# FFN input projections as one level of Strassen's product in a two-layer encoder kernel, with the weight blocks summed on GpSimd

## Chip, core and metric

The kernel runs on one core of one Trainium2 chip. The metric is the device time of one execution in microseconds (us). Before the change three runs gave 1635.26, 1635.56 and 1637.29 us; the median is 1635.56.

## What is computed

Two layers of an encoder on a sequence of 512 positions and 1024 channels, in float32. Each layer normalizes its input, projects it, runs three branches (attention, convolution, Fourier mixing), merges them through gates, projects with `w_out` and adds the residual. Then comes the feed-forward part (FFN), which the change is about:

```python
x = x + merged @ w_out[l]
h2 = rmsnorm(x, norm2_g[l])
f_gate, f_up = jnp.split(h2 @ w_ffn_in[l], 2, axis=-1)      # (512, 1024) @ (1024, 2*2816)
x = x + (jax.nn.silu(f_gate) * f_up) @ w_ffn_out[l]
```

## The kernel before

**Layout.** Activations lie transposed: a tile has 128 channels on its partitions and the 512 positions along its free side, so the 1024 channels are eight tiles (`KT`). A weight block is 128x128. All weights are packed on the host in the order of use, eight blocks to a chunk of 128x1024 elements (512 KB), 134 chunks to a layer.

**A product in float32 accuracy.** Weights and activations are split into a rounded high part and the rest. `chunk` (L185) loads a chunk to a tile `wr`, lets ScalarE (ACT) write the high part `wh` (L194) and VectorE (DVE) the rest `wl` (L195). `split` (L144) does the same for activations (L147 on ACT, L148 on DVE; with a scale L150 and L151). `gemm` (L208) multiplies one column block of weights with all tiles of the activation: for each 128-channel step three matmuls of 512 columns, high by high, high by rest and rest by high, all added up in one PSUM bank. Every matmul goes through `mm`, so all of them have line L114.

**The FFN.** After `w_out` (loop from L384, one product `ps` for each of eight tiles) the new residual `xt` is written by DVE (L391), scaled and split to the tiles `X` (L150, L151), and its squares are added up on GpSimd (POOL, L239). The inverse norm `rb2` (L420) is applied after the products. The 2816 hidden channels are 22 blocks (`NJ`); they are done in two runs of 11. For each block, called a unit here, there are two `gemm` calls with eight steps each, gate and up, which is 48 matmuls on two chunks of weights. `unit` (L399) multiplies the gate product with `rb2` (L401), applies Silu on ACT (L402), multiplies the up product with `rb2` (L404) and both together (L405), and splits the result (L147, L148). After the 11 units of a run, eight `gemm` calls with 11 steps each multiply the run's results with `w_ffn_out`, and DVE adds them to the residual (L426). So a layer has the order: `w_out`, units 0 to 10, output products, units 11 to 21, output products.

**What sets the order.** A scheduler puts the instructions of each engine into a fixed row before the program runs, by a priority that the kernel sets (`at`, with `self.t` as a running count of matmul time). Weight work is given a priority `WL` (16000 ns) ahead of its use. On the chip each engine takes its row strictly from front to back, and an instruction that has to wait holds up all behind it. Weight loads are issued from SyncE's row (SP). Tiles come from pools with a fixed number of buffers: `WB = (2, 3, 3)` for `wr`, `wh` and `wl`; a load waits until the last reader of the buffer's old content is done.

Of the kernel before, what the change touches and what calls it, by code (L numbers as in the profile page):

```python
# [9 lines left out]
F32 = mybir.dt.float32  # L10
# [6 lines left out]
P = 128  # L17
# [60 lines left out]
def lam_init(l):  # L78
    return 0.8 - 0.6 * math.exp(-0.3 * l)


class Hybrid:
# [267 lines left out]
    def main(self, l):  # L350
# [31 lines left out]
        x2, xg, acc = [], [], None  # L382
        g2 = self.par(l, "g2")
        for m in range(KT):  # L384
            xr = self.slot("M")
            self.at(self.t - 20000)
            getattr(nc, QS[3]).dma_start(xr, self.xin[m])
            self.at(self.t)
            ps = self.gemm(ms)
            xt = self.slot("V")  # L390
            nc.vector.scalar_tensor_tensor(out=xt, in0=ps, scalar=0.5, in1=xr, op0=ALU.mult, op1=ALU.add)  # L391
            xg.append(self.split_to(xt, "X", scale=g2[:, m : m + 1]))
            acc = self.sq_add(xt, acc, "M")
            x2.append(xt)
        self.xg, self.acc = [], None
        xin = []
        rb2 = None

        def unit(j, pg, pu):  # L399
            z = self.slot("M")  # L400
            nc.vector.tensor_tensor(out=z, in0=pg, in1=rb2, op=ALU.mult)  # L401
            nc.scalar.activation(z, z, AF.Silu)  # L402
            u = self.slot("M")
            nc.vector.tensor_tensor(out=u, in0=pu, in1=rb2, op=ALU.mult)  # L404
            nc.vector.tensor_tensor(out=u, in0=u, in1=z, op=ALU.mult)  # L405
# [535 lines left out]
def _pack(inp, l):  # L941
# [3 lines left out]
    def add(w):  # L945
        seq.append(_tiles(w).reshape(-1, P, P))
# [117 lines left out]
```

## Time and profile before

| | |
|---|---|
| runs | 1635.26, 1635.56, 1637.29 us |
| span of the profiled execution, first to last instruction | 1635.0 us |
| TensorE (PE) busy | 1618.7 us, 99% of the span |
| DVE busy | 1089.5 us, 67% |
| ACT busy | 678.2 us, 41% |
| POOL busy | 119.5 us, 7% |
| first layer: units 0 to 10, output products, units 11 to 21, output products | 474 to 592, to 652, to 771, to 832 us |

The own time of the profiled execution is not listed apart from its span; the median of the runs is 0.56 us above the span. Busy shares are means over stages: the units are only a part of each layer. DVE, ACT and POOL rows give the time an instruction took on its engine, including time in which it was held up after it had started. Ends of matmuls are modelled by the profiler, so the distance between two starts is what a matmul costs.

### The profile page before, as it was taken

How to read it: one execution, taken by the hardware profiler on the slowest of the kernel's cores; microseconds unless marked ns; L12 is line 12 of the kernel's file. 1: busy time of each engine (PE TensorE's matmuls, PEld its weight loads, DVE VectorE, ACT ScalarE, POOL GpSimd, SP SyncE). 2: the span in 40 equal slices, each digit the busy share in tenths (PEclk: the TensorE clock that was granted, in tenths of full speed). 3: DMA queues.
4: the chain of work that ended last, by engine and by line, in shares of the span. 5: the costliest groups of instructions: out<-in, count | busy, mean ns of one | idle time of the engine just before them, and what ended most of it. 6: DMA issues, size and time to landing. Idle time of an engine off the chain costs nothing.

```text
span 1635.0 us, 20023 instructions
## 1 busy us (share of the span) xinstructions
PE 1618.7 (99%) x7512; PEld 1340.8 (82%) x7512; DVE 1089.5 (67%) x1820; ACT 678.2 (41%) x1059; POOL 119.5 (7%) x85
## 2 busy tenths in 40 slices
PE   8999999999999999999999999999999999999999
PEld 6888888887888888888888888888878888888887
DVE  7999999896644433444459999998975444334432
ACT  5345555773443221323344464557634332223221
POOL 4000000112410000000100000001132000000000
PEclk9999999999999999999999999999999999999999
DMA  5545233322432323223343542332224223222332
GB/s 177 176 136 165 78 110 102 98 88 71 136 112 94 103 91 100 93 96 104 128 138 95 162 148 81 100 113 85 87 86 146 95 99 102 92 95 99 93 113 77
DMA packets 61439, 178.50 MB, mean 109 GB/s; under 512 B 8976, under 2 KB 9872, under 8 KB 61344
## 3 DMA queue, kind: packets, MB, share of 16 engines
q1 hardware_dynamic: 60912, 176.11, 33.3%
q0 software_dynamic: 432, 1.13, 0.3%
q8 instruction: 59, 0.97, 0.3%
q14 instruction: 36, 0.29, 0.1%
HBM read 163.30 MB, written 13.89 MB: 108 GB/s over the span
## 4 chain that ended last, share of the span: by engine, by line
PE 96%; ACT 2%; DVE 1%; DMA 0%; issue 0%; SPq 0%; DVEq 0%; ACTq 0%
PE main L114 83%; PE s L114 5%; PE att L114 3%; PE oth L114 3%; PE att L124 2%; DMA V<-in_xT 0%; PE att L583 0%; ACT at L691 0%; ACT cv L924 0%; DVE wl L195 0%; PE oth L124 0%; ACT wh L194 0%; DVE B L151 0%; ACT L924 0%; ACT L441 0%
## 5 line engine op out<-in xcount | busy, mean ns | idle before, releaser
L114 PE MATMUL main<-X,wh 128*128 128x512 f32 x2208 | 692.2, 391 | 0.0
L194 ACT CAST wh<-wr 128x1024 fp32r<-128x1024 f32 x268 | 281.7, 1052 | 649.5 <-PE main L114 375.6
L114 PEld LDWEIGHTS main<-X,wh 128*128 128x128 f32 x2208 | 413.4, 188 | 85.1 <-issue 0.5
L195 DVE TENSOR_TENSOR wl<-wr,wh 128x1024 fp32r<-128x1024 f32 x268 | 341.4, 1274 | 139.4 <-ACT wh L194 138.6
L114 PE MATMUL main<-X,wl 128*128 128x512 f32 x1104 | 431.7, 391 | 0.0
L114 PEld LDWEIGHTS main<-X,wl 128*128 128x128 f32 x1104 | 207.5, 188 | 42.7 <-issue 0.5
L867 DVE SCALAR_TENSOR_TENSOR cv<-cv,hcw,cv 128x497 f32<-128x497 f32 (+14 forms) x240 | 176.4, 735 | 1.2
L114 PE MATMUL main<-att,wh 128*128 128x512 f32 x384 | 119.6, 391 | 3.0 <-ACT att L147 3.0
L691 ACT ACTIVATE at<-s,mx 128x512 f32<-128x512 f32 x128 | 88.0, 688 | 78.6 <-DVE mx L689 63.0
L404 DVE TENSOR_TENSOR M<-main,rb 128x512 f32<-128x512 f32 x42 | 29.1, 692 | 133.8 <-PE main L114 133.8
L114 PE MATMUL main<-A,wh 128*128 128x512 f32 x320 | 106.4, 392 | 0.0
L114 PE MATMUL main<-wh,X 128*128 128x512 f32 x288 | 96.5, 391 | 0.0
L401 DVE TENSOR_TENSOR M<-main,rb 128x512 f32<-128x512 f32 x42 | 29.0, 691 | 91.0 <-PE main L114 91.0
L689 DVE TENSOR_REDUCE mx<-s 128x1 f32<-128x512 f32 x128 | 86.5, 679 | 4.3 <-PE s L114 4.0
L114 PEld LDWEIGHTS main<-att,wh 128*128 128x128 f32 x384 | 71.8, 188 | 19.2 <-ACT att L147 3.5
L114 PE MATMUL main<-act,wh 128*128 128x512 f32 x256 | 80.2, 394 | 0.0
L114 PE MATMUL main<-cv,wh 128*128 128x512 f32 x240 | 77.3, 392 | 1.1 <-ACT cv L147 1.1
L239 POOL TENSOR_TENSOR M<-M,M 128x512 f32<-128x512 f32 x28 | 46.9, 1675 | 421.0 <-ACT M L236 378.3
L114 PE MATMUL main<-att,wl 128*128 128x512 f32 x192 | 75.0, 391 | 0.0
L114 PE MATMUL main<-A,wl 128*128 128x512 f32 x192 | 74.9, 392 | 0.0
L114 PEld LDWEIGHTS main<-A,wh 128*128 128x128 f32 x320 | 59.8, 188 | 12.6 <-issue 0.5
L426 DVE TENSOR_TENSOR V<-main,V 128x512 f32<-128x512 f32 x32 | 22.1, 691 | 65.9 <-PE main L114 65.9
(223 smaller groups left out, 2260.9 us busy)
## 6 DMA issues: line engine op xcount, KB each, us to landing
wr<-in_w SPq DMA_DIRECT2D x268, 512.0 KB, 3.5
dqk<-at SPq DMA_DIRECT2D x32, 256.0 KB, 3.8
qst<-dqk SPq DMA_DIRECT2D x96, 64.0 KB, 1.9
kst<-dqk SPq DMA_DIRECT2D x96, 64.0 KB, 1.9
V<-in_xT SPq DMA_DIRECT2D x8, 256.0 KB, 7.6
att<-dftd SPq DMA_DIRECT2D x8, 256.0 KB, 4.2
M<-in_xT SPq DMA_DIRECT2D x8, 256.0 KB, 3.5
x<-V SPq DMA_DIRECT2D x8, 256.0 KB, 2.6
```

Source lines behind the costliest of these rows:

```text
L114: return self.pin(self.nc.tensor.matmul(out, lhsT=lhsT, rhs=rhs, start=start, stop=stop))
L124: self.pin(self.nc.tensor.transpose(ps[:, s], src[:, s], self.ident))
L194: nc.scalar.copy(hi, raw)
L195: nc.vector.tensor_tensor(out=lo, in0=raw, in1=hi.bitcast(F32), op=ALU.subtract)
L239: nc.gpsimd.tensor_tensor(out=sq, in0=acc, in1=sq, op=ALU.add)
L401: nc.vector.tensor_tensor(out=z, in0=pg, in1=rb2, op=ALU.mult)
L404: nc.vector.tensor_tensor(out=u, in0=pu, in1=rb2, op=ALU.mult)
L426: nc.vector.tensor_tensor(out=x2[m], in0=ps, in1=x2[m], op=ALU.add)
L689: nc.vector.tensor_reduce(out=mx, in_=ps, axis=AX.X, op=ALU.max, negate=True)
L691: nc.scalar.activation(e, ps, AF.Exp, bias=mx, accum_out=z1 if c else z0)
L867: ins = nc.vector.scalar_tensor_tensor(out=acc[:, a:b], in0=g[:, a + d : b + d], scalar=w[:, t : t + 1], in1=acc[:, a:b], op0=ALU.mult, op ...
```

## The change

The activation (1024 channels by 512 positions) and the weights of a unit (1024 by gate and up, 256 columns) are each cut into a grid of 2 by 2 blocks: channels in two halves of 512, positions in two halves of 256, weights in gate and up. One level of Strassen's product in Winograd's form then needs seven block products in place of eight, and sums of blocks before and after.

- `pair_weights` takes the place of the chunk loads of a unit. It loads the two chunks to `wr` tiles `r1` and `r2` (each holds two weight blocks of 128x512), makes three new sums `s1`, `s2`, `s4` and overwrites a part of `r1` with the fourth, `s3`. The four sums are `tensor_tensor` on GpSimd. The two `wr` tiles are split as before (`halves`), and `s1`, `s2`, `s4` are split as 128x512 tiles of their own (`single`, through `split`).
- `combine` makes the four sums of activation blocks on DVE while `w_out` is worked on, for each pair of channel tiles that belong together, and splits them. The order of the eight `w_out` products becomes 0, 4, 1, 5 and so on.
- `product` is one block product: four channel steps, three matmuls of 256 columns each. `pair_gemm` runs seven of them into two PSUM banks `b1` and `b2`. After the first four, ACT copies `b1` to `p15` and DVE adds `b2` to it; the last three are added into the banks.
- `unit` makes gate and up from `b1`, `b2` and the tile `qw` (which is `p15`) with three more sums of 256 columns.
- `WB` becomes (3, 4, 4), and weights of units get a priority 20000 ns ahead (`WLS`). Unit 0 of the first run is no longer held back until after unit 1.

The host packs the same weight blocks in another order. Line numbers of the changed kernel differ: L252 and L202 are the rest of a chunk, L154 and L155 stand for L147 and L148, L260 to L266 are the four weight sums, L281 the matmuls of `product`, L328 and L329 the copy and the sum to `p15`, L521 to L529 the DVE steps of `unit`, L509 stands for L391, and L295 to L298 are the sums of `combine`.

```diff
-WB = (2, 3, 3)
+WB = (3, 4, 4)
+WLS = 20000
+HALF = 108
...
+    def pair_weights(self, early):
...
+        self.at(self.t - WLS)
+        raws = []
+        for _ in range(2):
+            raw = self.wp.tile([P, CHUNK * P], F32, tag="raw", name=self.nm("wr"), bufs=WB[0])
...
+            nc.sync.dma_start(raw, self.a["w"][self.l, c])
...
+        r1, r2 = raws
+        a21, a11 = r1[:, 0:T], r1[:, T : 2 * T]
+        a22, a12 = r2[:, 0:T], r2[:, T : 2 * T]
...
+        g = nc.gpsimd.tensor_tensor
+        g(out=s1, in0=a21, in1=a22, op=ALU.add)
+        g(out=a21, in0=a11, in1=a21, op=ALU.subtract)
+        halves(("s3", "a11"), r1)
+        g(out=s2, in0=s1, in1=a11, op=ALU.subtract)
+        single("s1", s1)
+        single("s2", s2)
+        g(out=s4, in0=a12, in1=s2, op=ALU.subtract)
+        halves(("a22", "a12"), r2)
+        single("s4", s4)
...
+    def product(self, ps, w, xs, ks, start, stop):
...
+            for i, (a, b) in enumerate(((wh, xh), (wh, xl), (wl, xh))):
+                self.lastmm = self.pin(
+                    self.nc.tensor.matmul(
+                        ps, lhsT=a[:, s], rhs=b, start=start and k == ks[0] and i == 0,
...
+    def combine(self, ua, ub, t, tags):
...
+        v(out=t1, in0=ua[:, h:T], in1=ua[:, 0:h], op=ALU.subtract)
+        v(out=t3, in0=ub[:, h:T], in1=ua[:, h:T], op=ALU.subtract)
+        v(out=t2, in0=ub[:, h:T], in1=t1, op=ALU.subtract)
+        v(out=t4, in0=ub[:, 0:h], in1=t2, op=ALU.subtract)
...
+    def pair_gemm(self, u, w, xc, split_k=False):
...
+        first = (
+            (b1[:, 0:h], "a11", "b11", True), (b1[:, h:T], "s1", "t1", False),
+            (b2[:, h:T], "s3", "t3", True), (b2[:, 0:h], "s2", "t2", False),
+        )
...
+        p15 = self.slot("M")
+        nc.scalar.copy(p15, b1)
+        nc.vector.tensor_tensor(out=p15, in0=b2, in1=p15, op=ALU.add)
+        ks = list(range(n))
+        self.product(b1[:, 0:h], w["a12"], x("b21"), ks, False, False)
+        self.product(b1[:, h:T], w["s4"], x("b22"), ks, False, True)
+        self.product(b2[:, h:T], w["a22"], x("t4"), ks, False, True)
+        return b1, b2, p15
...
-        def unit(j, pg, pu):
+        def unit(j, b1, b2, qw):
             z = self.slot("M")
-            nc.vector.tensor_tensor(out=z, in0=pg, in1=rb2, op=ALU.mult)
+            v = nc.vector.tensor_tensor
+            v(out=z[:, 0:h], in0=b1[:, 0:h], in1=rb2[:, 0:h], op=ALU.mult)
+            v(out=z[:, h:T], in0=b1[:, h:T], in1=qw[:, 0:h], op=ALU.add)
+            v(out=z[:, h:T], in0=z[:, h:T], in1=rb2[:, h:T], op=ALU.mult)
             nc.scalar.activation(z, z, AF.Silu)
             u = self.slot("M")
-            nc.vector.tensor_tensor(out=u, in0=pu, in1=rb2, op=ALU.mult)
-            nc.vector.tensor_tensor(out=u, in0=u, in1=z, op=ALU.mult)
+            v(out=u[:, 0:h], in0=b2[:, h:T], in1=qw[:, 0:h], op=ALU.add)
+            v(out=u[:, h:T], in0=qw[:, 0:h], in1=qw[:, h:T], op=ALU.add)
+            v(out=u, in0=u, in1=rb2, op=ALU.mult)
+            v(out=u, in0=u, in1=z, op=ALU.mult)
...
-                held.append((j, self.gemm(xg, tag), self.gemm(xg, tag)))
+                w = self.pair_weights(half == 0 and j < 4)
+                got = self.pair_gemm(j, w, xc, half == 0 and j == 0)
```

Three places in the engines' fixed rows follow, of before and of the change. A name before the arrow is what is written, names behind it what is read; `main`, `s` and `att` are PSUM banks, `wr`, `wh`, `wl` weight chunks, `M` working tiles, `cv` the weight sums, `A` their split parts, `rb` the tile of `rb2`.

DVE, one unit in the first run, before: two PSUM steps, a product, a split and two chunks.

```order
L401 TENSOR_TENSOR M_5065<-main_5003,rb_4703 128x512
L195 TENSOR_TENSOR wl_5110<-wr_5107,wh_5109 128x1024
L404 TENSOR_TENSOR M_5068<-main_5034,rb_4703 128x512
L405 TENSOR_TENSOR M_5068<-M_5068,M_5065 128x512
L195 TENSOR_TENSOR wl_5151<-wr_5148,wh_5150 128x1024
L148 TENSOR_TENSOR kst_5072<-M_5068,qst_5071 128x512
```

DVE, the same place now: twelve of the fourteen steps of one round.

```order
L522 TENSOR_TENSOR M_5493<-main_5404,M_5454 128x256
L527 TENSOR_TENSOR M_5498<-M_5454 128x256
L155 TENSOR_TENSOR A_5656<-cv_5645,A_5655 128x512
L523 TENSOR_TENSOR M_5493<-M_5493,rb_4821 128x256
L526 TENSOR_TENSOR M_5498<-main_5405,M_5454 128x256
L528 TENSOR_TENSOR M_5498<-M_5498,rb_4821 128x512
L252 TENSOR_TENSOR wl_5665<-wr_5643,wh_5664 128x1024
L529 TENSOR_TENSOR M_5498<-M_5498,M_5493 128x512
L155 TENSOR_TENSOR A_5660<-cv_5646,A_5659 128x512
L252 TENSOR_TENSOR wl_5785<-wr_5775,wh_5784 128x1024
L329 TENSOR_TENSOR M_5588<-s_5539,M_5588 128x512
L155 TENSOR_TENSOR kst_5504<-M_5498,qst_5503 128x512
```

An L155 for `s4` and L521 stand ahead of the next L522 and complete the round; the step to `p15` (L329) stands right behind the chunk `wl_5785`, and only the last two rows and those two lie between that and L522.

POOL, from the last square sums of the first layer's `w_out` on, before: the next instruction belongs to the second layer.

```order
L239 TENSOR_TENSOR M_4550<-M_4508,M_4550 128x512
L239 TENSOR_TENSOR M_4592<-M_4550,M_4592 128x512
L239 TENSOR_TENSOR M_4634<-M_4592,M_4634 128x512
L239 TENSOR_TENSOR M_6671<-M_6622,M_6671 128x512
L239 TENSOR_TENSOR M_6727<-M_6671,M_6727 128x512
```

POOL, two units in the first run now: four sums to a unit with nothing between them.

```order
L260 TENSOR_TENSOR cv_5779<-wr_5775,wr_5777 128x512
L261 TENSOR_TENSOR wr_5775<-wr_5775 128x512
L263 TENSOR_TENSOR cv_5780<-cv_5779,wr_5775 128x512
L266 TENSOR_TENSOR cv_5781<-wr_5777,cv_5780 128x512
L260 TENSOR_TENSOR cv_5913<-wr_5909,wr_5911 128x512
L261 TENSOR_TENSOR wr_5909<-wr_5909 128x512
L263 TENSOR_TENSOR cv_5914<-cv_5913,wr_5909 128x512
L266 TENSOR_TENSOR cv_5915<-wr_5911,cv_5914 128x512
```

The chunk `wr_5775` is overwritten in part by the second sum, so its split (`wl_5785` in the row of DVE above) comes behind that sum.

PE, the start of a gate product before; it needs a chunk's two parts and nothing else.

```order
L114 MATMUL main_4962<-X_4630,wl_4966 128x512
L114 MATMUL main_5003<-X_4337,wh_5006 128x512 [waits DVE_49,Activation_49]
L114 MATMUL main_5003<-X_4338,wh_5006 128x512
L114 MATMUL main_5003<-X_4337,wl_5007 128x512 [waits DVE_49]
L114 MATMUL main_5003<-X_4378,wh_5006 128x512
```

PE, ahead of the seventh product of a unit now; `s_5538` and `s_5539` are its banks, `att_5672` the first bank of the next unit.

```order
L281 MATMUL s_5538<-B_4685,A_5535 128x256
L281 MATMUL att_5672<-at_4583,wh_5650 128x256 x2
L281 MATMUL att_5672<-at_4583,wl_5651 128x256
L281 MATMUL att_5672<-at_4682,wh_5650 128x256
L281 MATMUL s_5539<-X_4396,wh_5530 128x256 [waits DVE_49]
L281 MATMUL s_5539<-X_4397,wh_5530 128x256
```

The seventh product writes into `s_5539` and waits for DVE's step to `p15`, which reads that bank; a part of the next unit's first product stands ahead of it.

More of the change, by code (lines that the diff above doesn't have):

```diff
@@ new lines, in pair_gemm, with x @@
+    def pair_gemm(self, u, w, xc, split_k=False):
+        nc = self.nc
+        tag = ("s", "att", "main")[u % 3]
+        b1, b2 = self.bank(tag), self.bank(tag)
+        h = T // 2
+        n = len(xc)
+        def x(name):
+            return [p[name] for p in xc]
+        first = (
+            (b1[:, 0:h], "a11", "b11", True), (b1[:, h:T], "s1", "t1", False),
+            (b2[:, h:T], "s3", "t3", True), (b2[:, 0:h], "s2", "t2", False),
+        )
+        steps = (list(range(n - 1)), [n - 1]) if split_k else (list(range(n)),)
+        for ks in steps:
+            for i, (ps, a, b, start) in enumerate(first):
+                self.product(ps, w[a], x(b), ks, start and ks[0] == 0, i % 2 == 1 and ks[-1] == n - 1)
+        p15 = self.slot("M")
[6 more added lines that the diff above has]
+        return b1, b2, p15
@@ L381, in main @@
             ms.append(self.split_to(merged[m], "cv" if m < 4 else "A"))
-        x2, xg, acc = [], [], None
+        x2, xc, acc = [None] * KT, [], None
         g2 = self.par(l, "g2")
[L384 to L394, printed above, removed]
+        h = T // 2
+        for q in range(KT // 2):
+            us = self.wtp.tile([P, 2, T], F32, tag="wth", name=self.nm("us"))
+            ts = self.wtp.tile([P, 2, T], F32, tag="wtl", name=self.nm("ts"))
+            for i, m in enumerate((q, q + KT // 2)):
+                xr = self.slot("M")
+                self.at(self.t - 20000)
+                getattr(nc, QS[3]).dma_start(xr, self.xin[m])
+                self.at(self.t)
+                ps = self.gemm(ms)
+                xt = self.slot("V")
+                nc.vector.scalar_tensor_tensor(out=xt, in0=ps, scalar=0.5, in1=xr, op0=ALU.mult, op1=ALU.add)
+                nc.scalar.activation(us[:, i, :], xt, AF.Copy, scale=g2[:, m : m + 1])
+                acc = self.sq_add(xt, acc, "M")
+                x2[m] = xt
+            xc.append(self.combine(us[:, 0, :], us[:, 1, :], (ts[:, 0, :], ts[:, 1, :]), XCT[q]))
         self.xg, self.acc = [], None
@@ L414, in main @@
             act = []
-            held = []
             for j in range(NJ // 2):
-                tag = "s" if half == 0 and j == 0 else "main"
-                held.append((j, self.gemm(xg, tag), self.gemm(xg, tag)))
+                w = self.pair_weights(half == 0 and j < 4)
+                got = self.pair_gemm(j, w, xc, half == 0 and j == 0)
                 if half == 0 and j == 0:
                     rb2 = self.inv_rms(acc, D, "M", "rb")
-                    continue
-                while held:
-                    act.append(unit(*held.pop(0)))
+                act.append(unit(j, *got))
             for m in range(KT):
@@ L976, in _pack @@
         proj("w_proj_a", m)
-    add(inp["w_out"][l])
+    w = inp["w_out"][l]
+    for m in range(KT // 2):
+        for c in (m, m + KT // 2):
+            add(w[:, c * P : (c + 1) * P])
     w1, w2 = inp["w_ffn_in"][l], inp["w_ffn_out"][l]
@@ L980, in _pack @@
         for j in range(half * NJ // 2, (half + 1) * NJ // 2):
-            add(w1[:, j * P : (j + 1) * P])
-            add(w1[:, FF + j * P : FF + (j + 1) * P])
+            for k in range(2):
+                for o in (FF, 0):
+                    add(w1[k * D // 2 : (k + 1) * D // 2, o + j * P : o + (j + 1) * P])
         add(w2[half * FF // 2 : (half + 1) * FF // 2])
```

49 lines of the change are left out of this document (48 added, 1 removed).

## Prediction

> **What bounds the kernel now.** The page's busy times and its chain of work that ended last come first.
>
> ```profile
> PE 1618.7 (99%) x7512; PEld 1340.8 (82%) x7512; DVE 1089.5 (67%) x1820; ACT 678.2 (41%) x1059; POOL 119.5 (7%) x85
> PE 96%; ACT 2%; DVE 1%; DMA 0%; issue 0%; SPq 0%; DVEq 0%; ACTq 0%
> ```
>
> TensorE is the bound: 96% of the chain. The view by windows shows how the stages of the FFN differ from that mean: the first layer's first 11 units, and one unit alone (columns: PE, PEld, DVE, ACT, POOL busy, granted clock, DMA share, GB/s).
>
> ```profile
> 474.00:592.00 118.00, 118.00 (x520) 97.24 (x519) 57.59 (x70) 39.53 (x48) 0.00 (x0) 1.00 0.30 98
> 496.20:507.10 10.90, 10.90 (x50) 9.02 (x49) 5.04 (x6) 3.23 (x4) 0.00 (x0) 1.00 0.29 98
> ```
>
> Here PE never rests, DVE works 5.0 of 10.9 us, ACT 3.2 and POOL not at all. So fewer matmuls would shorten this stage for as long as the others can follow. The timeline of DVE in these units gives the pitch of a unit and of DVE's steps.
>
> ```profile
> 485.52 0.69 DVE L404 TENSOR_TENSOR M<-main,rb 128x512 f32<-128x512 f32 x1 [0.56 <-PE main L114]
> 486.25 0.69 DVE L405 TENSOR_TENSOR M<-M,M 128x512 f32<-128x512 f32 x1
> 486.86 1.22 DVE L195 TENSOR_TENSOR wl<-wr,wh 128x1024 fp32r<-128x1024 f32 x1
> 488.00 0.69 DVE L148 TENSOR_TENSOR act<-M,act 128x512 fp32r<-128x512 f32 x1
> ...
> 496.40 0.69 DVE L404 TENSOR_TENSOR M<-main,rb 128x512 f32<-128x512 f32 x1 [3.35 <-PE main L114]
> ...
> 507.28 0.69 DVE L404 TENSOR_TENSOR M<-main,rb 128x512 f32<-128x512 f32 x1 [3.31 <-PE main L114]
> ```
>
> A unit takes 496.40 - 485.52 = 10.88 us (507.28 - 496.40 again), which over 48 matmuls is 0.227 us for 512 columns. DVE starts an instruction before the last one has ended: after a 512-wide step of 0.69 the next starts 0.61 later (486.25 to 486.86), after a chunk of 1.22 it starts 1.14 later (486.86 to 488.00). Where a step needs the result of the one right ahead, it is 0.73 (485.52 to 486.25).
>
> **Matmuls: removed 48 of 512 columns, added 84 of 256.** Seven products of four channel steps with three matmuls are 84. The attention's second product already has 256 columns; the timeline of PE there:
>
> ```profile
> 178.56 0.29 PE L114 MATMUL att<-wtl,V 128*128 128x256 f32 x1
> 178.68 0.28 PE L114 MATMUL att<-wth,V 128*128 128x256 f32 x1
> ...
> 179.28 0.29 PE L114 MATMUL att<-wtl,V 128*128 128x256 f32 x1
> ```
>
> Start to start is 0.12 us (six steps in 0.72), more than half of 0.227. So 84 x 0.12 = 10.08 us a unit instead of 10.88: 0.80 saved, not an eighth (1.36). Over 44 units that is 35 us, if PE stays the bound.
>
> [...]
>
> **DVE: from six steps a unit to fourteen.** Counted from DVE's row of a unit: two chunks as before (2 x 1.14 = 2.28), seven steps of 512 (the rest of `s1`, `s2`, `s4` and of the activation, the sum to `p15`, `u` times `rb2`, `u` times `z`), 7 x 0.61 = 4.27, and five of 256. For these the nearest row is
>
> ```profile
> L717 DVE TENSOR_TENSOR ar<-att,ar x32: 393/412/419, 181.0 to 1198.0; 64x256 f32<-64x256 f32 x32
> ```
>
> 0.41 less the same 0.08 of overlap is 0.33 to 0.34, so 1.70. Together 8.25 us, and 8.5 with two steps that need the one right ahead (2 x 0.12). Alone DVE would still fit into 10.08.
>
> **POOL: from nothing to four sums a unit.** The source view of the branch merge has the same instruction:
>
> ```profile
> L453 POOL TENSOR_TENSOR B<-B,M x16: 1275/1289/1737, 344.8 to 1202.1; 128x512 f32<-128x512 f32 x16
> L453 POOL TENSOR_TENSOR B<-B,A x16: 1293/1672/2277, 405.5 to 1228.7; 128x512 f32<-128x512 f32 x16
> ```
>
> At 1.29 us four take 5.2, which fits. But what DVE does meanwhile is the point. First a single meeting, in the timelines of DVE and POOL, then a row of four POOL sums at the end of the branches.
>
> ```profile
> 388.55 2.31 DVE L195 TENSOR_TENSOR wl<-wr,wh 128x1024 fp32r<-128x1024 f32 x1
> 388.50 1.29 POOL L453 TENSOR_TENSOR B<-B,M 128x512 f32<-128x512 f32 x1 [7.18 <-DVE M L452]
> ...
> 406.45 1.41 DVE L195 TENSOR_TENSOR wl<-wr,wh 128x1024 fp32r<-128x1024 f32 x1
> 407.79 1.77 DVE L148 TENSOR_TENSOR cv<-B,cv 128x512 fp32r<-128x512 f32 x1
> 409.48 0.68 DVE L452 SCALAR_TENSOR_TENSOR A<-A,main 128x512 f32<-128x512 f32 x1
> 410.08 1.19 DVE L148 TENSOR_TENSOR cv<-B,cv 128x512 fp32r<-128x512 f32 x1
> 411.19 2.30 DVE L195 TENSOR_TENSOR wl<-wr,wh 128x1024 fp32r<-128x1024 f32 x1
> 405.49 6.93 POOL L453 TENSOR_TENSOR B<-B,A 128x512 f32<-128x512 f32 x4 [9.26 <-DVE A L452]
> ```
>
> A chunk of 1.22 took 2.31, longer by 1.09, because a POOL sum had started 0.05 us ahead. In the second place five DVE steps that alone take 1.14 + 3 x 0.61 + 1.22 = 4.19 us take 7.04 (406.45 to 413.49), while POOL's first sum ends and three more run whole: 2.85 more, 0.95 a sum. The two engines take turns. L452, which reads PSUM, is not held (0.68). Of DVE's fourteen steps only four read PSUM (`p15`, L521, L522, L526).
>
> [...]
>
> When do the four sums run? The second chunk of a unit's weights gets the buffer that DVE frees with the L252 right ahead of L329 (rows of the order above), and a load takes
>
> ```profile
> wr<-in_w SPq DMA_DIRECT2D x268, 512.0 KB, 3.5
> ```
>
> So the sums start about 3 us behind L329. By then L521 and L522 are through (0.61 for the activation's rest, 0.61 for `s4`, 2 x 0.34), and of the steps on PSUM only L526 falls into a sum. The sums meet the steps on SBUF: four times 1.0, less 0.34 for L526: 3.7 us. DVE's round is 8.5 + 3.7 = 12.2 us. That is over PE's 10.08, and PE's seventh product waits for L329, which stands behind all this. DVE becomes the bound, PE rests 2 us in each unit.
>
> ACT gets a copy and three casts more; with Silu and the activation's cast these are six 512-wide steps beside the two chunks:
>
> ```profile
> L194 ACT CAST wh<-wr 128x1024 fp32r<-128x1024 f32 x268 | 281.7, 1052 | 649.5 <-PE main L114 375.6
> 497.93 0.62 ACT L147 CAST act<-M 128x512 fp32r<-128x512 f32 x1 [0.70 <-DVE M L405]
> ```
>
> 2 x 1.05 + 6 x 0.62 = 5.8 us, hidden in either round. SP's row has the same 134 loads a layer, none of them behind other waits than before; DMA is busy 0.30. Free.
>
> **Which units.** The sums that run in the round of unit j are those of unit j + 3. So of 11 units in a run eight rounds have sums, the last three have none and go at PE's 10.08. A run changes by 8 x (12.2 - 10.88) - 3 x 0.80 = 10.6 - 2.4 = +8.2 us. Four runs: +32.6.
>
> **The `w_out` stage.** DVE's four sums and their splits for each pair of tiles have room except behind the last product, where before there were three steps:
>
> ```profile
> 462.89 0.69 DVE L391 SCALAR_TENSOR_TENSOR V<-main,M 128x512 f32<-128x512 f32 x1 [2.65 <-PE main L114]
> 463.79 1.22 DVE L195 TENSOR_TENSOR wl<-wr,wh 128x1024 fp32r<-128x1024 f32 x1 [0.21 <-ACT wh L194]
> 464.94 0.74 DVE L151 SCALAR_TENSOR_TENSOR X<-V,par,X 128x512 fp32r<-128x512 f32 x1
> ```
>
> That chain took 2.8 us (462.89 to 465.68). Now there are eight steps, two of 512 and one chunk, three of 256, two more of 512: 0.61 x 4 + 1.14 + 3 x 0.34 = 4.6, with 0.24 for steps in line 4.8. Unit 0 does the first three pairs of its first four products meanwhile, 36 x 0.12 = 4.3. The sums of unit 2 fall into the same time, up to 3 x 1.0. Between 0 and 3.5 us a layer; I take 3, since POOL's row has three sums there: +6 in all.
>
> **The sum.** Span 1635.0 + 32.6 + 6 = 1673.6; the median of the runs lay 0.56 above the span, so 1674.
>
> **Rivals.**
>
> *PE stays the bound.* The sums find gaps in DVE's row, a round stays under 10.08. For it: DVE was idle for over half of these units, and the meeting above shows a step on PSUM running through. Against it: with 8.5 us of its own DVE may lose no more than 1.6 a unit, 0.4 a sum, less than half of any meeting on SBUF in this trace. From that point PE decides; time 1635.6 - 35 + 6 = 1607. Chance 0.14.
>
> *The gain and the loss even out.* A loss of 0.6 a sum gives a round of 10.9, and 8 x 0.02 - 2.4 = -2.2 a run: 1635.6 - 9 + 6 = 1633, no change (within 0.2%, some 3 us, about what a measurement of this kernel can tell). Chance 0.06.
>
> *A unit's weights come late.* Load, two sums, cast and rest are a chain: 3.5 + 2 x 1.29 + 1.05 + 1.22 = 8.4 us, with two turns lost to DVE about 10. If PE had to wait for the split sums in each unit because nothing is prepared ahead, the 3.7 us that DVE loses would add to PE's 10.08 instead of lying beside it, and the round would be 13.8: 8 x 2.9 - 2.4 = 21 a run, 1635.6 + 84 + 6 = 1725. Against it: in DVE's row the split weights stand a unit ahead of their matmuls. Chance 0.10.
>
> **Chances and range.** The forecast, DVE's rounds with POOL's sums as the bound, has the remaining 0.70, nearly all of it slower. Faster by over 0.2%: 0.15; within 0.2%: 0.05; slower: 0.80. The price of a sum is between nothing (beside steps on PSUM) and its whole 1.29 us. At 0.75 a sum the round is 11.5, a run 8 x 0.62 - 2.4 = +2.6 and the time 1652; at 1.29 the round is 13.7, a run 8 x 2.8 - 2.4 = +20 and the time 1722. I reach below to 1622, which is a round of 10.6 and 0.52 a sum, and above to 1715, a round of 13.5. Left out are the fast rival and most of the late weights, under 2 in 10.
>
> **What would show it.** Right: in a unit's window PE is busy about 10 of 12.2 us, DVE without gaps, and the largest waits of the first layer's units end with L329; L252 and L155 in these units have means of 1.6 to 2.3 and near 1.2 to 1.7 us where they meet POOL, steps on PSUM keep theirs; the first run takes 474 to about 603. Matmuls of 256 columns start 0.12 apart. Wrong: PE without gaps, units of 10.1 us and DVE's means as before (the fast rival); waits of PE that end with L155 of a weight sum or with ACT's casts behind POOL (late weights); L252 unchanged beside POOL sums would break the turn-taking itself.

## The result, and the profile after

The changed kernel takes 1703.04 us (median of four runs, 1702.30 to 1704.83), the kernel before 1635.93 us beside it: a ratio of 1.0412 with a 95% interval of 1.0397 to 1.0427, 67 us slower. The forecast was 1674, its range 1622 to 1715: right in sign and mechanism, too small by 29 us. The profiled execution took 1702.3 us, 2.1 more than its span.

The page of the changed kernel, busy times and chain:

```profile
PE 1625.8 (96%) x9096; PEld 1419.3 (83%) x9096; DVE 1426.2 (84%) x2220; ACT 791.7 (47%) x1267; POOL 411.8 (24%) x261
PE 75%; DVE 17%; issue 4%; ACT 2%; DMA 1%; POOL 1%; SPq 0%; DVEq 0%; POOLq 0%; ACTq 0%
```

TensorE's share of the chain fell from 96% to 75%, and DVE has 17%. TensorE executes 1584 matmuls more (in a unit 84 of 256 columns for 48 of 512), and its busy time is no less: in parts of the span its granted clock was 0.50, as windows below show (0.975 in the mean, 0.998 before). The window of one unit in the second run of the first layer (columns as before):

```profile
722.30:734.60 12.30, 11.58 (x84) 11.58 (x84) 12.27 (x15) 5.14 (x8) 6.77 (x4) 0.86 0.30 85
```

84 matmuls now fill 12.30 us. DVE is busy 12.27 of them, ACT 5.14, POOL 6.77 with the four sums. The timelines of DVE and POOL, one round earlier:

```profile
700.99 0.41 DVE L526 TENSOR_TENSOR M<-main,M 128x256 f32<-128x256 f32 x1
701.44 1.71 DVE L528 TENSOR_TENSOR M<-M,rb 128x512 f32<-128x512 f32 x1
703.07 2.31 DVE L252 TENSOR_TENSOR wl<-wr,wh 128x1024 fp32r<-128x1024 f32 x1
705.32 1.78 DVE L529 TENSOR_TENSOR M<-M,M 128x512 f32<-128x512 f32 x1
707.02 1.78 DVE L155 TENSOR_TENSOR A<-cv,A 128x512 fp32r<-128x512 f32 x1
708.72 1.21 DVE L252 TENSOR_TENSOR wl<-wr,wh 128x1024 fp32r<-128x1024 f32 x1
```

```profile
701.33 1.28 POOL L260 TENSOR_TENSOR cv<-wr,wr 128x512 f32<-128x512 f32 x1 [5.67 <-DMA wr<-in_w]
...
706.62 1.63 POOL L266 TENSOR_TENSOR cv<-wr,cv 128x512 f32<-128x512 f32 x1
```

From 701.33 to 708.25 POOL sums. The four DVE steps that start in that time take 1.71, 2.31, 1.78 and 1.78 us; the same L252 without a sum beside it (708.72) takes 1.21, and a 512-wide step 0.68 (L329 below). The excess over these, 1.03 + 1.10 + 1.10 + 1.10, is 4.3 us for four sums. L526, which reads PSUM, is nearly through here when the first sum starts. In other rounds it lies wholly inside a sum (15 of its 44 steps), and none of its steps is longer for it, as the range of its durations over the whole span shows (shortest, median and longest in ns; the rows of the other two banks end at 426 and 415):

```profile
L526 DVE TENSOR_TENSOR M<-s,M x16: 410/414/426, 491.9 to 1627.1; 128x256 f32<-128x256 f32 x16
```

The row of DVE's own view of L329 gives the length of all rounds of a run, by the first and the last start of each of its three forms: in the second run of layer 1, then in the first.

```profile
L329 DVE TENSOR_TENSOR M<-s,M x4: 678/678/682, 672.2 to 779.9; 128x512 f32<-128x512 f32 x4
L329 DVE TENSOR_TENSOR M<-att,M x4: 678/679/684, 685.0 to 789.4; 128x512 f32<-128x512 f32 x4
L329 DVE TENSOR_TENSOR M<-main,M x3: 678/678/678, 697.3 to 771.6; 128x512 f32<-128x512 f32 x3
```

```profile
L329 DVE TENSOR_TENSOR M<-s,M x4: 678/680/691, 483.1 to 591.5; 128x512 f32<-128x512 f32 x4
L329 DVE TENSOR_TENSOR M<-att,M x4: 678/681/684, 492.6 to 601.0; 128x512 f32<-128x512 f32 x4
```

Ten rounds take 789.4 - 672.2 = 117.2 us and 601.0 - 483.1 = 117.9. The waits of TensorE in the second run all end with that step:

```profile
PE att L281 <- DVE M L329: 4.7, 3, 2.1
PE main L281 <- DVE M L329: 2.9, 3, 1.9
PE s L281 <- DVE M L329: 2.8, 2, 2.0
```

The engines took their rows in order here: DVE's steps above start in the order of its row, and TensorE, idle for 2.10 us up to 723.02, went on with the matmul that waited for L329.

Where the time went, by the start of DVE's last step (L426 before, L547 now) of each run of output products: each column is the time from the one before it, the first from the start of the span. This table also carries the experiments below.

| kernel | us | layer 1 to the end of run 1 | run 2 | layer 2 to the end of run 1 | run 2 |
|---|---|---|---|---|---|
| before | 1635.9 | 644.0 | 180.2 | 626.9 | 180.2 |
| changed | 1703.0 | 665.2 | 188.4 | 654.6 | 188.4 |
| sums on DVE | 1622.2 | 641.5 | 171.4 | 632.6 | 171.4 |
| no sums | 1607.6 | 634.2 | 171.4 | 625.1 | 171.4 |
| stores in place of sums | 1608.2 | 633.6 | 171.4 | 626.2 | 171.4 |
| sums on both engines | 1782.6 | 691.6 | 201.1 | 682.7 | 201.8 |
| before, buffer counts alone | 1644.7 | 645.8 | 180.2 | 634.6 | 180.2 |
| scale read from PSUM | 1682.8 | 658.7 | 183.3 | 651.2 | 183.8 |
| early sums on DVE | 1686.5 | 654.5 | 190.1 | 646.0 | 189.9 |

The second runs are longer by 8.2 and 8.1 us; the forecast had 8.2 for each run. The stretches that contain `w_out` and a first run are longer by 21.2 and 27.7, where it had 3 + 8.2 = 11.2 for each. So the missing 26 us of span lie in these two stretches: 10 us in layer 1, 16.5 in layer 2.

### The profile page after: what moved, and what is told of

It reads as the page before. It is cut to its first block, busy times and chain, and to the rows that moved or that the text cites. A ratio compares the mean times of both kernels' runs of the same rounds, so it can differ in the third digit from the quotient of the medians.

```text
span 1700.2 us, 24154 instructions
## 1 busy us (share of the span) xinstructions
PE 1625.8 (96%) x9096; PEld 1419.3 (83%) x9096; DVE 1426.2 (84%) x2220; ACT 791.7 (47%) x1267; POOL 411.8 (24%) x261
## 4 chain that ended last, share of the span: by engine, by line
PE 75%; DVE 17%; issue 4%; ACT 2%; DMA 1%; POOL 1%; SPq 0%; DVEq 0%; POOLq 0%; ACTq 0%
PE main L121 51%; PE s L281 5%; PE att L281 4%; PE s L121 4%; PE att L121 3%; DVE M L529 3%; PE main L281 3%; DVE wl L252 3%; PE oth L121 3%; DVE A L155 3%; PE att L131 2%; DVE att L155 1%; DVE M L329 1%; DMA wr<-in_w 1%; DVE M L523 1%
## 5 line engine op out<-in xcount | busy, mean ns | idle before, releaser
L202 DVE TENSOR_TENSOR wl<-wr,wh 128x1024 fp32r<-128x1024 f32 x180 | 233.0, 1295 | 74.6 <-ACT wh L201 73.9
L121 PE MATMUL main<-X,wh 128*128 128x512 f32 x864 | 277.4, 395 | 0.0
L121 PEld LDWEIGHTS main<-X,wh 128*128 128x128 f32 x864 | 161.4, 189 | 32.8 <-issue 0.5
L121 PE MATMUL main<-X,wl 128*128 128x512 f32 x432 | 170.9, 396 | 0.0
L252 DVE TENSOR_TENSOR wl<-wr,wh 128x1024 fp32r<-128x1024 f32 x88 | 141.2, 1605 | 5.5 <-ACT wh L251 5.4
L1019 POOL TENSOR_TENSOR cv<-cv,cv 128x512 f32<-128x512 f32 x6 | 9.8, 1630 | 515.6 <-DVE cv L988 515.6
L260 POOL TENSOR_TENSOR cv<-wr,wr 128x512 f32<-128x512 f32 x36 | 53.4, 1485 | 298.0 <-DMA wr<-in_w 254.9
L155 DVE TENSOR_TENSOR A<-cv,A 128x512 fp32r<-128x512 f32 x108 | 108.7, 1008 | 13.2 <-ACT A L154 12.9
L154 ACT CAST A<-cv 128x512 fp32r<-128x512 f32 x108 | 65.4, 617 | 65.8 <-PE s L281 22.9
L121 PEld LDWEIGHTS main<-X,wl 128*128 128x128 f32 x432 | 81.6, 189 | 17.1 <-issue 0.5
L547 DVE TENSOR_TENSOR V<-main,V 128x512 f32<-128x512 f32 x32 | 22.1, 690 | 77.5 <-PE main L121 77.5
```

The costliest lines, as they stand in the source:

```text
L121: return self.pin(self.nc.tensor.matmul(out, lhsT=lhsT, rhs=rhs, start=start, stop=stop))
L154: self.lasthi = nc.scalar.copy(hi, src)
L155: nc.vector.tensor_tensor(out=lo, in0=src, in1=hi.bitcast(F32), op=ALU.subtract)
L202: nc.vector.tensor_tensor(out=lo, in0=raw, in1=hi.bitcast(F32), op=ALU.subtract)
L252: nc.vector.tensor_tensor(out=lo, in0=src, in1=hi.bitcast(F32), op=ALU.subtract)
L260: g(out=s1, in0=a21, in1=a22, op=ALU.add)
```

## Experiments

The theory is that of the forecast: GpSimd's sums and DVE's steps on SBUF take turns, DVE's round grows over TensorE's, and DVE is the bound. One rival is that DVE is too full with its own fourteen steps, whoever makes the sums. The other is that the chain of load, sums, cast and split is too long on GpSimd and each unit's weights come late.

**All four sums on DVE.**

```diff
-        g = nc.gpsimd.tensor_tensor
+        g = nc.vector.tensor_tensor
```

> The four weight sums of a unit are DVE instructions instead of POOL instructions; nothing else is edited. Theory 1 (DVE and POOL take turns on SBUF, and DVE's round is the bound): a round of DVE loses the holds and gains four steps of 0.61 and two short waits, 8.5 + 2.4 + 0.3 = 11.2 us instead of 12.3. Four runs with eight such rounds: 32 x 1.1 = 35 less, and the start of a first run (DVE held by POOL sums there) some 5 less in each layer: about 1658. L252 back at 1.2 us, L155 at 0.68. Theory 2 (DVE's own fourteen steps and their waits are the bound, POOL's sums lie beside them): four steps more, 12.3 + 2.4 = 14.7, about 1780. Theory 3 (a unit's split weights come too late for PE because of the chain load, sums, cast, rest): the chain gets shorter by 4 x 0.7, rounds of 10 to 11, between 1635 and 1660; waits of PE end with weight tiles, not with L329.

Measured: 1622.19 us (1621.86 to 1622.69), ratio to before 0.9913, interval 0.9896 to 0.9929. One word makes a kernel that is 14 us faster than the one before and 81 us faster than the changed one. DVE's groups of the second run:

```profile
L252 DVE TENSOR_TENSOR wl<-wr,wh 128x1024 fp32r<-128x1024 f32 x19 | 23.0, 1219 | 0.1
...
L260 DVE TENSOR_TENSOR cv<-wr,wr 128x512 f32<-128x512 f32 x9 | 6.2, 687 | 5.1 <-DMA wr<-in_w 5.1
```

A sum takes DVE 0.69 us, and with the overlap of 0.08 its row moves on by 0.6. On GpSimd the same sum costs DVE about 1.1 in the round shown above. The engine that was to be relieved has less to do when it does the work itself: over the whole span DVE is busy 1364.9 us here and 1426.2 in the changed kernel. The theory of turns holds in sign, but its number was too high: DVE's 8.5 + 4 x 0.6 = 10.9 us in a unit with sums is over TensorE's 10.08, yet the second run takes 171.4 us, as little as without any sums (the next experiment), and TensorE waits 1.0 us in all of it (641 to 813 us). Split weights that lie ready for more than one unit would let longer rounds and the last ones without sums even out; that is argued from these numbers and not shown by itself. The 14.8 us by which the span is longer than without sums lie in the stretches with the first runs. The window of the ten rounds of the second run (PE, PEld, DVE, ACT, POOL):

```profile
646.80:750.30 103.50, 102.45 (x842) 101.61 (x841) 99.06 (x169) 51.60 (x76) 0.00 (x0) 1.00 0.34 104
```

DVE is busy 9.9 us a round and TensorE 10.2 of 10.35.

**No sums.** The splits read raw blocks in place of `s1`, `s2`, `s3` and `s4`, so the weight sums are left out of the computation.

```diff
-        g(out=s1, in0=a21, in1=a22, op=ALU.add)
-        g(out=a21, in0=a11, in1=a21, op=ALU.subtract)
...
-        g(out=s2, in0=s1, in1=a11, op=ALU.subtract)
-        single("s1", s1)
-        single("s2", s2)
-        g(out=s4, in0=a12, in1=s2, op=ALU.subtract)
+        single("s1", a21)
+        single("s2", a11)
...
-        single("s4", s4)
+        single("s4", a12)
```

> The four weight sums are left out: s1, s2, s4 are split straight from blocks of the loaded chunks and s3 is the block a21, so the FFN's values are not the reference's. POOL does nothing for the units; DVE, ACT and PE have all their other instructions. Theory 1: DVE's round is 8.5 and PE's 9.5 (84 matmuls in the last round of a run after the change took 9.51), PE is the bound: 44 x (10.88 - 9.5) = 61 less than before, some 3 more at each start of a first run, and up to 7 for the wait in the second layer's branches: 1580 to 1590. Theory 2 (DVE's own steps): rounds stay near 12, 1690 or more. Theory 3 (late weights): without the sums the chain is load, cast, rest, 6 us, so about as theory 1.

Measured: 1607.55 us in one run. DVE's step to `p15` has line L322 in this kernel; its timeline in the second run, and the window of the round between:

```profile
680.89 0.68 DVE L322 TENSOR_TENSOR M<-att,M 128x512 f32<-128x512 f32 x1
690.97 0.69 DVE L322 TENSOR_TENSOR M<-main,M 128x512 f32<-128x512 f32 x1
```

```profile
680.90:691.00 10.10, 10.10 (x87) 10.10 (x86) 8.43 (x16) 5.40 (x8) 0.00 (x0) 1.00 0.36 109
```

The pitch is 10.08 us, 84 x 0.12, with TensorE always busy, and DVE's own steps take 8.43: both are the forecast's numbers (10.08 and 8.5). So the rival of a DVE too full by itself falls. The time is above what was expected, because a round takes 10.08 us and not the 9.5 taken there: 35.2 saved by TensorE and 8.1 paid for the buffers (below) make 1636.2 - 35.2 + 8.1 = 1609.

**Stores in place of sums.** GpSimd writes constants to the same four places, in the same order and with the same buffers; the sums are left out again.

```diff
-        g = nc.gpsimd.tensor_tensor
+        def g(out, in0, in1, op):
+            nc.gpsimd.memset(out, 0.5)
```

> Each POOL sum is a POOL memset of the same 128x512 target: same place in the chain, same waits, but it reads nothing; the values are not the reference's. Theory 1 with a hold only where POOL reads SBUF: L252 stays at 1.2 us beside the memsets, and the time is that of the kernel without sums, 1580 to 1595. Theory 1 with a hold by any POOL instruction: L252 is longer by about the memset's own time, rounds between 10 and 12.3, 1600 to 1700. Theory 3 (late weights through the chain over POOL): hardly faster than with the sums, 1680 to 1703, with DVE's steps at their own length.

Measured: 1608.18 us in one run, as without sums, and like that run above the range expected. GpSimd's group in the whole run, then DVE's groups from 640 to 760 us:

```profile
L260 POOL MEMSET cv<- 128x512 f32 x108 | 55.8, 526 | 189.6 <-DVE A L155 189.4
```

```profile
L252 DVE TENSOR_TENSOR wl<-wr,wh 128x1024 fp32r<-128x1024 f32 x18 | 22.0, 1222 | 6.3 <-ACT wh L251 6.3
L155 DVE TENSOR_TENSOR A<-cv,A 128x512 fp32r<-128x512 f32 x28 | 19.2, 685 | 0.0
```

L252 and L155 keep 1222 and 685 ns. So GpSimd's instruction in the chain, its row and its buffers don't hold DVE; what is left is its reading. But the store is also shorter (0.53 us against 1.28 and more), so this run alone does not clear the chain of a long GpSimd step. The next one does.

**Sums on both engines.** DVE makes the sums, and for each GpSimd adds two blocks of the same weights to a tile that nobody reads.

```diff
-        g = nc.gpsimd.tensor_tensor
+        gv = nc.vector.tensor_tensor
+        def g(out, in0, in1, op):
+            gv(out=out, in0=in0, in1=in1, op=op)
+            nc.gpsimd.tensor_tensor(out=self.spare, in0=r2[:, 0:T], in1=r2[:, T : 2 * T], op=ALU.add)
...
+            self.spare = cp.tile([P, T], F32, tag="spare", name="spare")
```

> The weight sums are on DVE as in the first experiment, and POOL additionally does four sums a unit of a unit's second chunk into a tile that nobody reads. Only the load buffer waits for them. Theory 1: DVE is held by them as by the real ones, a round of 11.2 + 3.7 = 14.9; 32 rounds: about 1658 + 118 = 1776. Theories 2 and 3: POOL's instructions that nobody waits for cost nothing, the same time as the sums on DVE alone.

Measured: 1782.64 us in one run, 160 more than with the sums on DVE alone, or 160.5 / 176 = 0.91 us for each sum that does nothing. No weight waits for the result of these, so the chain rival falls, and the price of a turn is measured by itself: the forecast had 0.95 to 1.09. DVE's own busy time over the whole span grows from 1364.9 to 1535.6 us, 0.97 for each sum. (DVE's first sums wait 5.2 us for loads in the window below, 5.1 without the idle sums, so it isn't the raw buffers that they hold up.) DVE's groups from 690 to 830 us (L262 are DVE's sums here):

```profile
L252 DVE TENSOR_TENSOR wl<-wr,wh 128x1024 fp32r<-128x1024 f32 x19 | 25.8, 1365 | 0.0
...
L262 DVE TENSOR_TENSOR cv<-cv,wr 128x512 f32<-128x512 f32 x9 | 13.8, 1532 | 0.0
...
L262 DVE TENSOR_TENSOR cv<-wr,wr 128x512 f32<-128x512 f32 x9 | 7.7, 852 | 5.2 <-DMA wr<-in_w 5.2
```

The holding has moved with the sums: they now meet DVE's own sums (1532 ns for a step of 687) and L252 less (1365; over the whole span of the changed kernel its mean is 1605).

**The buffer counts alone.** The kernel before, with `WB = (3, 4, 4)` and the smaller DMA scratch of the changed one, which makes room for them.

```diff
-WB = (2, 3, 3)
+WB = (3, 4, 4)
...
-    nc = bacc.Bacc("TRN2", target_bir_lowering=False, num_devices=1)
+    nc = bacc.Bacc("TRN2", target_bir_lowering=False, num_devices=1, dynamic_dma_scratch_size=2048)
```

> The kernel before, with the buffer counts of the changed one alone (WB (3, 4, 4) and the smaller DMA scratch): no sums, no seven products. Theory 'buffers reorder the branches': the stall of about 7 us in the second layer's branches (matmul gaps of 3.3, 1.5, 1.5 and 1.2 us, then a halved clock) shows here too, since the scheduler sees other buffers; 1640 to 1643 us against 1636. Rival 'the stall belongs to the new product' (its sums, its weight order, its tail): 1635 to 1637 us, without these gaps.

Measured: 1644.73 us (1642.97 to 1646.39), ratio 1.0047, interval 1.0030 to 1.0063: 8.1 us slower. The profiled execution is the slowest of the four; of the 9.5 us by which its span is longer, the table puts 7.7 into the stretch that holds layer 2's branches and 1.8 into the first. TensorE's waits in the branches, in this kernel from 1135 to 1152 us and in the changed one from 1160 to 1180:

```profile
PE s L114 <- ACT at L691: 2.7, 3, 1.3
PE main L114 <- ACT cv L147: 2.5, 1, 2.5
```

```profile
PE main L121 <- ACT cv L154: 2.8, 1, 2.8
PE s L121 <- ACT at L812: 2.8, 3, 1.3
```

They are the same waits; in the kernel before TensorE has only two waits of 0.2 us each between 1130 and 1180 us. The order of TensorE's row has changed: attention products come ahead of projections that used to cover the conv norm, and TensorE waits for the norm. That the scheduler places weight work earlier when it has more buffers is the likely reason, which no run shows. The product of seven isn't needed for it. Whether the counts or the scratch do it was not separated.

**The scale read from PSUM.** ACT copies the tile of `rb2` to a PSUM bank, and L523 and L528 read it there.

```diff
+                    rbp = self.bank("oth")
+                    nc.scalar.copy(rbp, rb2)
...
-            v(out=z[:, h:T], in0=z[:, h:T], in1=rb2[:, h:T], op=ALU.mult)
+            v(out=z[:, h:T], in0=z[:, h:T], in1=rbp[:, h:T], op=ALU.mult)
...
-            v(out=u, in0=u, in1=rb2, op=ALU.mult)
+            v(out=u, in0=u, in1=rbp, op=ALU.mult)
```

> The changed kernel, but the scale by 1/rms in L523 and L528 is read from a copy in PSUM, so that these two DVE steps have only one operand in SBUF; the GpSimd sums stay. Theory 'only DVE steps with two SBUF operands take turns with GpSimd's sums': L528 falls from 1155 ns to about 700, L523 to about 420, the sums find some 1.1 us more per unit beside which they run free, the round of a unit with sums falls from 12.3 to 11.3 to 11.8, and the time to 1670 to 1690 us. Rival 'any DVE step that reads SBUF is held' or 'the chain of sums and splits sets the round': L528 still over 1 us, the round still 12.3, 1698 to 1708 us.

Measured: 1682.84 us (1682.36 to 1684.56), ratio 1.0285, interval 1.0270 to 1.0300: 20 us less than the changed kernel, with the same sums. The groups of DVE:

```profile
L529 DVE TENSOR_TENSOR M<-M,M 128x512 f32<-128x512 f32 x44 | 62.9, 1430 | 0.4
L528 DVE TENSOR_TENSOR M<-M,oth 128x512 f32<-128x512 f32 x44 | 30.2, 685 | 1.2
```

and of the changed kernel, where L529 has the same 62.9 us in all:

```profile
L528 DVE TENSOR_TENSOR M<-M,rb 128x512 f32<-128x512 f32 x44 | 50.8, 1155 | 1.2
```

L528 falls from 1155 to 685 ns, L529 with both operands in SBUF stays at 1430, and the round falls from 12.4 us to 11.74, by two starts in this kernel's timeline of DVE:

```profile
712.92 0.68 DVE L329 TENSOR_TENSOR M<-att,M 128x512 f32<-128x512 f32 x1
...
724.66 0.68 DVE L329 TENSOR_TENSOR M<-main,M 128x512 f32<-128x512 f32 x1
```

So DVE's steps with one operand in SBUF and one in PSUM were not held here: L528 keeps a mean of 685 ns and L523 one of 409 (512 in the changed kernel), and at 717.10 an L528 took 0.69 us beside a sum on GpSimd (716.71, 1.30 us). L529 with both operands in SBUF was held by sums (1430), and GpSimd's stores, which read nothing, held neither L252 nor L155 (1222 and 685 ns above). A held step doesn't lose the whole length of a sum: 0.91 to 1.10 us is lost, and the shortest sums take 1.28. Why it is less stays open.

**The early sums on DVE.** The sums of the first four units of each layer are made by DVE, the other 18 units' by GpSimd.

```diff
-        g = nc.gpsimd.tensor_tensor
+        g = (nc.vector if early else nc.gpsimd).tensor_tensor
```

> The changed kernel, with the sums of the first four units of each layer (those made ready during the w_out stage and the start of the first run) on DVE; the other seven units of the first run and all of the second keep theirs on GpSimd. Theory 'the excess over the forecast is the start of each first run, where GpSimd's sums hold combine's SBUF steps and the weights of two units have to be caught up': the w_out stage comes back by 4 to 6 us per layer and the first run by 4 to 8, 1677 to 1690 us. Rival 'only the number of sums beside DVE counts, wherever they lie': 32 of 176 sums leave GpSimd at 0.27 us each gained (0.95 lost beside a sum against 0.685 for one done on DVE), 1692 to 1697 us.

Measured: 1686.47 us (1686.02 to 1687.63), ratio 1.0306, interval 1.0291 to 1.0322. Moving 32 of 176 sums gives back 16.6 us, against 9 if only their number counted (32 x 0.27). The ten rounds of layer 1 keep about their length (116.4 us in the first run, 118.9 in the second, which gives 1.7 back without a known reason), but the first of them starts at 473.9 instead of 483.1 us. So the gain lies ahead of the rounds. TensorE's waits for the splits of `combine` from 455 to 482 us, here and then in the changed kernel:

```profile
PE s L281 <- DVE B L155: 0.3, 1, 0.3
PE s L281 <- ACT B L154: 0.2, 1, 0.2
```

```profile
PE s L281 <- DVE B L155: 2.9, 1, 2.9
PE s L281 <- DVE X L155: 2.2, 1, 2.2
PE s L281 <- ACT B L154: 2.0, 1, 2.0
```

In the changed kernel unit 0 waits 7.1 us for the last block sums of `combine` and their splits. DVE's timeline there shows why:

```profile
475.38 1.48 DVE L298 TENSOR_TENSOR ts<-us,ts 128x256 f32<-128x256 f32 x1
476.79 1.75 DVE L155 TENSOR_TENSOR B<-ts,B 128x512 fp32r<-128x512 f32 x1
```

Steps of 0.41 and 0.68 take 1.48 and 1.75, one turn each, because the sums of unit 2 and the square sums run on POOL. And TensorE's granted clock was 0.50 around two of these rests, of 2.15 us up to 466.19 and of 2.89 up to 478.59 (eighth column):

```profile
467.10:470.50 3.40, 3.37 (x17) 3.08 (x15) 3.26 (x5) 2.48 (x4) 1.28 (x1) 0.50 0.32 72
477.30:484.10 6.80, 5.51 (x20) 4.47 (x21) 5.20 (x6) 3.52 (x6) 2.38 (x2) 0.50 0.00 0
```

Of these 10.2 us TensorE is busy 8.9. In proportion to the clock the same matmuls would take half of that at 1.00: another 4.4 us lost, by this estimate.

**Two raw buffers.** All sums on DVE and `WB = (2, 4, 4)`, against the stall in the branches.

```diff
-WB = (3, 4, 4)
+WB = (2, 4, 4)
```

> All four sums on DVE (as in the run with the sums on DVE, 1622.2 us), and two raw weight buffers instead of three (WB (2, 4, 4)). Theory 'buffers reorder the branches': the order of the second layer's branches changes again, and part of the 7 us stall goes, 1615 to 1620 us, if two raw buffers still bring the weights in time (a chunk lands 3.6 us after its issue, and a unit takes two in 10 us). Rival 'third raw buffer needed': each unit with sums waits 1 to 2 us for its second chunk, 1630 to 1680 us.

Measured: 1661.83 us (1659.93 to 1668.69), ratio 1.0162, interval 1.0140 to 1.0185; the rival was right. DVE's and then TensorE's waits from 655 to 785 us:

```profile
DVE cv L260 <- DMA wr<-in_w: 10.8, 9, 1.8
```

```profile
PE att L281 <- DVE wl L252: 5.4, 2, 2.7
```

Nine first sums wait for their second chunk, 1.2 us each and 1.8 at most, and TensorE for the split behind. The third raw buffer is needed, and the stall stays: TensorE waits 4.4 and 1.7 us in the branches of layer 2.

**Three high buffers, and three of both.** All sums on DVE.

```diff
-WB = (3, 4, 4)
+WB = (3, 3, 4)
```

> All four sums on DVE, with three buffers instead of four for the high parts (WB (3, 3, 4)). The theory that the buffer counts reorder the second layer's branches: that order becomes another one, in which more products lie ahead of the conv norm's wait, so that 4 to 7 of the 8 us that the counts (3, 4, 4) cost come back; 1615 to 1619 us, if three high buffers suffice (a unit holds two at once). Rival 'the fourth high buffer carries the prefetch': the first sums of the next unit start only when a unit ends, PE waits 1 to 2 us in the units with sums, 1635 to 1680 us.

> All four sums on DVE, with three buffers for high and for low parts (WB (3, 3, 3)). As for the run with (3, 3, 4): 1615 to 1619 us if the branches alone change; 1635 to 1680 us if the prefetch of a unit's weights needs the fourth buffers.

Measured: 1628.54 us (1628.17 to 1629.17; ratio 0.9956, interval 0.9944 to 0.9969) with (3, 3, 4), and 1626.00 us (1625.46 to 1629.74; ratio 0.9945, interval 0.9933 to 0.9958) with (3, 3, 3). Both expectations missed: the runs lose less than the rival said (second run of layer 1: 175.9 and 176.5 us against 171.4), and the stall in the branches does not go. With (3, 3, 4), from 1125 to 1150 us:

```profile
PE main L121 <- ACT cv L154: 4.8, 1, 4.8
```

The order does change: the wait for the conv norm is now 4.8 us, beside one of 1.3 for attention (4.3 alone with (3, 3, 3)). The counts (3, 4, 4) stay the best of those that ran; how to have them without the stall is open.

**One sum on GpSimd.** `s1` on GpSimd, the other three on DVE.

```diff
-        g(out=s1, in0=a21, in1=a22, op=ALU.add)
+        nc.gpsimd.tensor_tensor(out=s1, in0=a21, in1=a22, op=ALU.add)
```

> Three of the four sums on DVE, the first one (s1) on GpSimd, with buffers (3, 4, 4). Theory 'a sum on GpSimd takes more of DVE's time (0.9 to 1.0 us) than one that DVE does itself (0.685 us)': slower than with all four on DVE, by 0.2 to 0.3 us in the 44 units and the wait for GpSimd's longer sum in front of the others; 1625 to 1640 us against 1622. Rival 'GpSimd takes load off DVE as long as its share is small': 1610 to 1620 us.

Measured: 1628.03 us (1627.54 to 1628.76), ratio 0.9953, interval 0.9938 to 0.9968, against 0.9896 to 0.9929 with all four on DVE: slower by some 6 us, in the direction that the theory of turns had. Even one sum of four on GpSimd does not help here. But the loss is not the theory's 0.2 to 0.3 us in each of 44 units: all of it lies in the stretches with the first runs (644.7 and 635.0 us against 641.5 and 632.6), and the second runs, in which TensorE is the bound, take 171.4 in both.

## Why the prediction came out as it did

- **Matmuls.** 84 x 0.12 = 10.08 us a unit: measured 10.08 without sums. Right.
- **DVE's fourteen steps.** 8.5 us: measured 8.43 busy in a round without sums. Right.
- **Turns.** 0.95 to 1.09 a sum was taken from a different place of the program; the sums that do nothing cost 0.91 each in time and 0.97 of DVE's, the sums in the round above up to 1.10. Steps that read PSUM keep 0.41 and 0.68, as forecast. Right. The 1.29 at the upper end of the forecast's prices, a whole sum lost, no run shows: the longest L252, L523, L528 and L529 of the changed kernel lose 1.10 to 1.11 us (2320, 1521, 1780 and 1786 ns, against 1207, 408, 678 and 679 for the shortest).
- **The round and the runs.** 12.2 us, eight of them, +8.2 a run: eight rounds take 12.4 (672.2 to 771.6), ten rounds 117.2 where the forecast's add up to 8 x 12.2 + 2 x 10.08 = 117.8, and the second runs are 8.2 and 8.1 longer. The mechanism is right, and that TensorE waits for L329 is what its waits say.
- **Luck in the totals.** That they agree to half a microsecond is partly luck. The turns cost 4.3 us and not 3.7, because the sums start 3.7 to 4.1 us behind L329, where the forecast had about 3, and L526 is mostly through by then; DVE's own steps, without gaps, leave 8.1 of the 12.4 and not 8.5. The eight rounds with sums are 1.8 us longer than forecast, and the last two take 17.8 where it had 20.2, probably because a part of their matmuls is done ahead. The first run of layer 1 has the same total from uneven rounds, 9.5 to 15.2 us with sums. In the window of a unit TensorE is not busy 10 of 12.2 us, as forecast, but 11.58 of 12.30, at a clock of 0.86.
- **When the first run ends.** The forecast had 603 us, from a table in which units 0 to 10 take 474 to 592. TensorE's unit matmuls there run from 462.7 to 583.2 us; in the changed kernel they run from 462.0 to 606.4. So the run with its start grew by 24 us, not by 11.
- **The `w_out` stage.** Forecast 3 us a layer; mis-sized. Waits of 7.1 us and 4.4 us of half clock make 11.5; the first L329 of layer 1 comes at 483.1 us, and at 471.3 in the kernel without sums. The step that failed is the price of three turns at 1.0 each behind the last product: there are more turns (sums of `combine`, their splits, three sums of unit 2 and POOL's own square sums), in a stretch in which TensorE has nothing else to do, and its granted clock is 0.50 in 10.2 us of it. The early sums on DVE take this back, 16.6 us for two layers.
- **The other stages.** Forecast 0, by silence: the counts in `WB` were read as a property of the units alone. They are shared with every product of the kernel, and in layer 2's branches they cost 7.7 us without any other part of the change. This is the only term whose mechanism the forecast did not have.
- **The sum.** The spans differ by 65.2 us: 38.6 forecast, about 9 more at each start of a first run and 7.7 in the branches make 64. The medians differ by 67.1, since the profiled executions are not the median ones. The 0.56 us that the forecast added to the span was 2.1 in this execution.
- **The rivals.** TensorE as the bound (1607) is what remains when the sums don't read SBUF on GpSimd: 1607.6 and 1608.2. The number is met by luck: the 6 us that it had for `w_out` did not come there, and the buffer counts cost 8.1. Late weights did not occur with three raw buffers.

What the forecast did not ask is what the sums cost on the engine next door. Its own rows had the answer: 0.61 for a 512-wide DVE step, 0.95 to 1.09 for a turn.

## What to carry to other kernels

Before work is moved from DVE to GpSimd to relieve DVE, compare two prices in the trace: what the step costs DVE itself (0.6 us here) and what a GpSimd step that reads SBUF takes from DVE in turns (0.9 to 1.1); if the second is larger, the move loads the engine that it was to relieve. Where GpSimd must do it, let DVE read one operand from PSUM meanwhile (L528 fell from 1155 to 685 ns here), and keep it out of stretches in which TensorE waits for DVE (16.6 us back here). Test a change of shared buffer counts by itself, since a scheduler can pay for it in a stage that the change does not touch (7.7 us here).

## What the hardware showed beyond that

Behind some rests of 2 to 4 us TensorE's granted clock was 0.50, inside a stage in which TensorE is busy 108.3 of 119.7 us (485.0 to 604.7). TensorE's timeline in the first run of layer 1:

```profile
540.83 0.88 PE L281 MATMUL main<-X,A 128*128 128x256 f32 x6
541.55 0.52 PE L281 MATMUL main<-B,A 128*128 128x256 f32 x3
...
546.63 0.79 PE L281 MATMUL main<-X,wh 128*128 128x256 f32 x2 [4.08 <-DVE M L329]
547.22 0.41 PE L281 MATMUL main<-X,wl 128*128 128x256 f32 x1
547.43 0.63 PE L281 MATMUL main<-X,wh 128*128 128x256 f32 x2
```

Ahead of the wait of 4.08 us six matmuls start in 0.72 us, 0.12 apart; behind it they start 0.21 apart (547.22 and 547.43). The granted clock is 1.00 from 538.9 to 542.3 us and 0.50 from 545.6 to 552.4. Behind a shorter rest it was 0.50 too: in the second run the windows

```profile
719.70:723.10 3.40, 1.30 (x12) 1.09 (x10) 3.40 (x4) 1.53 (x3) 0.98 (x1) 0.99 0.25 102
723.10:726.50 3.40, 3.40 (x16) 3.40 (x17) 3.37 (x9) 0.73 (x1) 0.42 (x1) 0.50 0.56 154
```

show TensorE busy 1.30 of 3.40 us, and then 3.40 us at 0.50. The rest in the first of them is one of 2.10 us, up to 723.02. It was not so behind every rest of that length: behind one of 2.02 us in the same run, up to 747.71, matmuls kept starting 0.12 apart (granted clock 1.00 from 747.7 to 757.0), and behind one of 1.93 us, up to 697.99, they did so for about 1.2 us and then started 0.21 apart (0.50 from 700 to 702). What decides between them the runs don't show. In these rounds it cost little, since DVE set their length; at the start of the first run of layer 1 it made 7.1 us of waits into a loss of about 11.5, by the estimate above.
